# A decoder step on one core: cache pages copied to a DRAM buffer by SyncE instead of gathered by GpSimd

## The chip, the cores and the metric

The kernel runs on 1 core of one Trainium2 chip. The metric is the device time of one execution in microseconds (us), the median of 3 runs. The engines are named as in the profile: PE (TensorE matmuls), PEld (its weight loads), DVE (VectorE), ACT (ScalarE), POOL (GpSimd), SP (SyncE, which here only issues transfers).

## The reference

The reference is one inference step of a two-layer decoder for one prompt of 256 tokens and 8 samples of 4 new tokens each, so 288 tokens in all. A layer is

```
x = x + 1/2 * SwiGLU1(RMSNorm(x))
h = RMSNorm(x);  p = h @ w_in
branches on h: gated DeltaNet | short conv | MLA | memory cross-attention
x = x + W_o( sum_b sigmoid(gate_b(h)) * branch_b )
x = x + 1/2 * SwiGLU2(RMSNorm(x))
```

The part that the change is about is the MLA branch of the samples. Each sample has a past of 2048 tokens in 16 pages of 128 tokens, found through a page table:

```
c_all = concat([ckv_pool[layer, pages].reshape(-1, 256), c_new])   # latent keys/values
r_all = concat([kr_pool[layer, pages].reshape(-1, 32),  r_new])    # rope keys
k = rmsnorm(concat([c_all @ w_uk per head, r_all]))                # 8 heads
p = softmax(q . k * scale, masked);  out = (p @ c_all) @ w_uv
```

All is fp32; the layers' outputs, the new states and the new cache rows are returned.

## The kernel before

Every large product is made of three fp32r matmuls: operands are split into a high and a low part, and `mm3` (L261 to L263) adds high·high, low·high and high·low. The weights come as 470 raw tiles `wraw` of 128x1024 (512 KB). SP loads them in a fixed order (`Stream.load`, L146) into four buffers; ACT makes the high part `wh` (L159) and DVE the low part `wl` (L160). So the weight stream passes SP, ACT and DVE ahead of each matmul on PE, and a raw tile is loaded as soon as DVE has made the last `wl` from the tile four before it.

A layer has these stages (times of layer 0 in the trace): FFN1 (7 to 215 us), stage AB with the memory branch and the convolutions (215 to 390), stage C with the MLA projections and the prompt's attention (390 to 525), stage D with the delta rule and the samples' paged attention (526 to about 935), then `wo` and FFN2. Layer 1 lies 1194 us later. A list of steps per stage is interleaved by hand, and a scheduler then orders the instructions of each engine by data and by its own estimate of when each is ready; so a change of what one engine issues can change the order on others.

What the prediction speaks of:

- `mem_prep` (L423 to L442), at the start of AB, loads the memory's eight tiles `mt` (128 KB each, two buffers, L426). For each, ACT makes `mh`, DVE makes `ml` (L429) and adds its square to `macc` (L241); L437 sums `macc` on PE. A tile's load has to wait until the tile two before it has been read.
- `mem_values` (L556 to L566), at the end of AB, loads for each of 8 samples a 512-KB tile `kc` (L561, two buffers), and PE makes 8 small matmuls with it into `accp` (L566).
- In D each page is used twice. Its transposed form `ct` (256 gathers of 128 KB) and the rope keys `kT` (64 gathers of four pages) are fetched by `page_fetch` (L1094) as indirect transfers issued by POOL (L1091). ACT and DVE split `ct` into `ch` and `cl`, and PE makes the keys `pgps`. The plain form `cn` is loaded by SP through `load_page` (L1203), with the page's number read into a register first.
- Every transfer of SP stands in one queue, in order, and takes one of eight semaphores in turn (DMAHW0 to DMAHW7), each free again when the transfer eight before has landed.

Of the kernel before, what the change touches and what calls it, by code (L numbers as in the profile page):

```python
# [28 lines left out]
PT, PSUB = T + 4, SUB + 4  # L29

# [3 lines left out]
    ("blk4", 4), ("i32s", 32), ("bmp", 8), ("hm", 4), ("sel", 2), ("cs", T), ("kt", T), ("iota", 1), ("iota32", 1),  # L34
# [98 lines left out]
class Stream:  # L133


    def __init__(self, nc, raw_pool, split_pool, dram, plan, ahead=3, raw_ahead=3):
        self.nc, self.rp, self.sp, self.dram, self.plan = nc, raw_pool, split_pool, dram, plan
        self.pos = self.n_sub = self.n_raw = 0
        self.ahead, self.raw_ahead = ahead, raw_ahead
        self.raw, self.sub = {}, {}  # L140
        self.total_raw = dram.shape[0]

    def load(self, upto):
# [34 lines left out]
def program(tc, I, O):  # L178
# [15 lines left out]

    base = pool("base")
# [121 lines left out]

    def ffn(n, ka, kb, nxt):
# [3 lines left out]
        for j in range(NFF):  # L322
            pg = proj(ka, j, KD, n.hi, n.lo)
            g = mk(fp, [128, T], "fg", bufs=2)
            mul(g, pg, n.r)
            act(g, g, AF.Silu)
            pu = proj(ka, NFF + j, KD, n.hi, n.lo)
            u = mk(fp, [128, T], "fu", bufs=2)
            mul(u, pu, n.r)
            mul(u, u, g)  # L330
            split(ah[:, j, :], al[:, j, :], u)
        ins = nc.scalar.preload_act_table_set("natural_log_exp_and_others")
        tc.keep_in_program_order(ins)
        for m in range(KD):
            ps = proj(kb, m, NFF, ah, al)
            STT(out=x[:, m, :], in0=ps, scalar=0.5, in1=x[:, m, :], op0=ALU.mult, op1=ALU.add)
            if nxt is not None:
                nxt.tile(m)
            else:
                nc.sync.dma_start(O["y"][:, m, :], x[:, m, :])  # L340
        fp.release()

    def mix(l, n, nxt):
# [289 lines left out]
        n_phys = I["ct"].shape[0] // (depth * 128)  # L633
        idx, idx4 = mk(ma, [128, NB * NPG], "idx", I32), mk(ma, [128, NB * 4], "idx4", I32)
        off = mk(ma, [128, 2], "off")
        TS_(out=off[:, 0:1], in0=C("iota"), scalar1=float(l * n_phys * 128), scalar2=None, op0=ALU.add)
        TS_(out=off[:, 1:2], in0=C("iota32"), scalar1=float(l * n_phys * 32), scalar2=None, op0=ALU.add)
        TS_(out=idx, in0=pti, scalar1=128.0, scalar2=off[:, 0:1], op0=ALU.mult, op1=ALU.add)
        TS_(out=idx4, in0=pt4, scalar1=32.0, scalar2=off[:, 1:2], op0=ALU.mult, op1=ALU.add)
# [442 lines left out]

        core = delta()
# [111 lines left out]
        loads = []  # L1195

        def load_page(dst, pg):
            ld, (page,) = nc.values_load_multi_w_load_instructions(
                pti[0:1, pg:pg + 1], engines=[mybir.EngineType.SP], min_val=0, max_val=n_phys - 1)
            if len(loads) > 3:  # L1200
                tc.add_manual_dep(ld[0].ins, loads[-4].ins.name, mybir.DependencyInfo(
                    mybir.DependencyClass.NoSync, mybir.DependencyReason.DATA), reason="registers")
            loads.append(nc.sync.dma_start(dst, I["cn"][l, bass.ds(page, 1), :, :].rearrange("o p c -> (o p) c")))  # L1203

        def values(b, qd):
# [7 lines left out]
            for i in range(2):  # L1213
                cn = mk(sa, [128, 2, 257], "cn", bufs=3)
                nc.vector.memset(cn[:, :, 256:257], 1.0)
                for j in range(2):
                    load_page(cn[:, j, 0:256], b * NPG + qd * 4 + i * 2 + j)
# [40 lines left out]

        mhl = []
# [17 lines left out]
    for k in range(KD):  # L1277
        nc.sync.dma_start(x[:, k, :], I["x"][:, k, :])
        if k == 1:
            W.load(1)  # L1280
    n = Norm(0, "g_f1")
# [5 lines left out]
    for m in range(KD):  # L1287
# [3 lines left out]
    pti = mk(base, [128, NB * NPG], "pti", I32)  # L1291
    nc.sync.dma_start(pti, I["pt"].rearrange("(o n) -> o n", o=1).to_broadcast([128, NB * NPG]))

    pt4 = mk(base, [128, NB * 4], "pt4")
    pt4t = mk(base, [128, NB * 4, 4], "xs")
    TT(out=pt4t, in0=pti.rearrange("p (q j) -> p q j", j=4), in1=C("blk4").unsqueeze(1).to_broadcast([128, NB * 4, 4]),
       op=ALU.mult)
    nc.vector.tensor_reduce(out=pt4, in_=pt4t, axis=AX.X, op=ALU.add)
    n.finish()
    for l in range(depth):  # L1300
# [11 lines left out]
    for p in (psb, psa, psm, wsp, wraw, base):  # L1312
# [3 lines left out]
def constants():  # L1316
# [41 lines left out]
    c["iota"][:, 0] = i  # L1358
    c["iota32"][:, 0] = i % 32
# [5 lines left out]
def layout(a):  # L1365
# [58 lines left out]
    f["ct"] = ct.reshape(-1, 256)  # L1424
    f["krt"] = a["cache_mla_krope"].transpose(0, 1, 3, 2).reshape(-1, 128)
# [46 lines left out]
```

## Time and profile before

| | |
|---|---|
| runs | 2417.37, 2409.87, 2414.66 us; median 2414.66 |
| profiled execution | 2407.3 us, its span 2405.3 us |
| mean granted clock of PE | 0.99 |
| busy share of the span | PE 96%, PEld 90%, DVE 66%, ACT 55%, POOL 15% |
| chain that ended last | PE 91%, DVE 3%, ACT 2%, DMA 2%, issue 2% |
| DMA | 149 GB/s over the span |

PE is busy nearly all the time, so the table alone says little about a change that touches no matmul. The profile has to be read by stage: where PE has gaps, how long each is, and which engine or transfer ended it. In the windows PEclk is the granted clock as a share of the full one.

### The profile page before, as it was taken

What the parts mean: (1) busy time and instruction counts of PE and PEld (TensorE: products, weight loads), DVE (VectorE), ACT (ScalarE), POOL (GpSimd) and SP (SyncE); (2) the same over time, 40 slices, a digit from 0 to 9 for tenths busy, and PEclk for the clock granted to TensorE, in tenths of its full rate; (3) what the DMA queues carried; (4) which work ended last, traced back from release to release, by engine and by line L of the source; (5) the groups of instructions that cost most, each with busy time, mean ns of one, the idle gap of its engine ahead of it and who ended that gap; (6) DMA issues with size and microseconds to landing.
All of it is one profiled execution on the core that took longest, in us unless ns stands there. A gap on an engine that the chain in (4) does not pass through costs nothing.

```text
span 2405.3 us, 50145 instructions
## 1 busy us (share of the span) xinstructions
PE 2310.6 (96%) x18368; PEld 2153.4 (90%) x18368; DVE 1597.9 (66%) x3484; ACT 1333.8 (55%) x3489; POOL 350.8 (15%) x461
## 2 busy tenths in 40 slices
PE   8999999999889999999999999999998899999999
PEld 8999898978767888999999998998887678889999
DVE  6666897675556655766566668876754666567664
ACT  5555756754445655655455557566544466556553
POOL 0000110113334430000000001101133344200000
PEclk9999999999999999999999999999999999999999
DMA  6555655431244445555555556553322444355554
GB/s 235 167 167 179 211 180 177 123 118 52 82 138 133 123 135 159 162 167 167 167 167 167 167 171 219 192 166 116 116 60 75 151 121 138 118 154 162 167 170 136
DMA packets 134949, 359.16 MB, mean 149 GB/s; under 512 B 19312, under 2 KB 56880, under 8 KB 134704
## 3 DMA queue, kind: packets, MB, share of 16 engines
q1 hardware_dynamic: 120368, 318.19, 42.2%
q0 software_dynamic: 14336, 37.77, 5.5%
q8 instruction: 146, 2.39, 0.4%
q14 instruction: 99, 0.81, 0.1%
HBM read 346.82 MB, written 9.06 MB: 148 GB/s over the span
## 4 chain that ended last, share of the span: by engine, by line
PE 91%; DVE 3%; ACT 2%; DMA 2%; issue 2%; another core or an unknown queue 0%; SPq 0%; ACTq 0%; DVEq 0%
PE mmps L261 20%; PE mmps L262 20%; PE mmps L263 19%; PE pgps L261 6%; PE pgps L263 6%; PE pgps L262 5%; PE accp L1220 2%; PE axp L864 2%; DMA mt<-in_mem 1%; PE axp L683 1%; ACT wh L159 1%; PE axp L1164 1%; DVE mx L1177 1%; PE axp L371 0%; DMA kc<-in_mem_v 0%
## 5 line engine op out<-in xcount | busy, mean ns | idle before, releaser
L159 ACT CAST wh<-wraw 128x512 fp32r<-128x512 f32 x940 | 580.1, 619 | 607.2 <-PE mmps L262 551.2
L160 DVE TENSOR_TENSOR wl<-wraw,wh 128x512 fp32r<-128x512 f32 x940 | 648.3, 691 | 344.9 <-ACT wh L159 296.6
L261 PE MATMUL mmps<-xh,wh 128*128 128x288 f32 x2512 | 751.6, 299 | 9.1 <-ACT wh L159 8.0
L262 PE MATMUL mmps<-xl,wh 128*128 128x288 f32 x2512 | 748.5, 298 | 0.0
L263 PE MATMUL mmps<-xh,wl 128*128 128x288 f32 x2512 | 741.9, 295 | 0.1
L261 PEld LDWEIGHTS mmps<-xh,wh 128*128 128x128 f32 x2512 | 473.7, 189 | 22.5 <-ACT wh L159 10.8
L262 PEld LDWEIGHTS mmps<-xl,wh 128*128 128x128 f32 x2512 | 475.2, 189 | 3.5 <-issue 1.4
L263 PEld LDWEIGHTS mmps<-xh,wl 128*128 128x128 f32 x2512 | 474.5, 189 | 3.5 <-issue 1.6
L261 PE MATMUL pgps<-mvh,ch 128*128 128x272 f32 x1024 | 316.7, 309 | 28.5 <-ACT s L1156 22.2
L1091 POOL DMA_INDIRECT ct<-in_ct,idx x256 | 249.3, 974 | 582.0 <-DVE cl L258 161.7
L244 ACT ACTIVATE sq<-pgps 128x256 f32<-128x256 f32 x512 | 193.6, 387 | 221.4 <-PE pgps L263 165.6
L262 PE MATMUL pgps<-mvl,ch 128*128 128x272 f32 x1024 | 301.2, 294 | 0.0
L263 PE MATMUL pgps<-mvh,cl 128*128 128x272 f32 x1024 | 300.9, 294 | 0.0
L261 PEld LDWEIGHTS pgps<-mvh,ch 128*128 128x128 f32 x1024 | 196.6, 192 | 63.6 <-ACT s L1156 35.6
L1157 DVE TENSOR_REDUCE ssum<-sq 128x8 f32<-128x512 f32 x256 | 173.6, 680 | 110.6 <-ACT sq L244 99.0
L261 PE MATMUL mmps<-ah,wh 128*128 128x288 f32 x704 | 207.7, 295 | 0.0
L263 PE MATMUL mmps<-ah,wl 128*128 128x288 f32 x704 | 207.6, 295 | 0.0
L262 PE MATMUL mmps<-al,wh 128*128 128x288 f32 x704 | 207.3, 294 | 0.0
L262 PEld LDWEIGHTS pgps<-mvl,ch 128*128 128x128 f32 x1024 | 197.1, 193 | 2.4 <-issue 1.4
L263 PEld LDWEIGHTS pgps<-mvh,cl 128*128 128x128 f32 x1024 | 196.4, 192 | 2.1 <-issue 0.7
L261 PEld LDWEIGHTS mmps<-ah,wh 128*128 128x128 f32 x704 | 132.4, 188 | 0.0
L262 PEld LDWEIGHTS mmps<-al,wh 128*128 128x128 f32 x704 | 132.4, 188 | 0.0
(407 smaller groups left out, 3376.6 us busy)
## 6 DMA issues: line engine op xcount, KB each, us to landing
wraw<-in_w SPq DMA_DIRECT2D x470, 512.0 KB
cn<-in_cn SPq DMA_DIRECT2D x256, 128.0 KB
kc<-in_mem_k SPq DMA_DIRECT2D x16, 512.0 KB
kc<-in_mem_v SPq DMA_DIRECT2D x16, 512.0 KB
ct<-in_ct,idx POOLq DMA_INDIRECT x256
S<-in_dn_S SPq DMA_DIRECT2D x8, 512.0 KB
out_s_S<-S SPq DMA_DIRECT2D x8, 512.0 KB
mt<-in_mem SPq DMA_DIRECT2D x16, 128.0 KB
```

The lines of the kernel that those rows point to most:

```text
L159: nc.scalar.copy(h, src)
L160: nc.vector.tensor_tensor(out=lo, in0=src, in1=h.bitcast(F32), op=ALU.subtract)
L244: nc.scalar.activation(out=out, in_=in_, func=f, **kw)
L261: MMUL(ps, wh, xh, start=first, stop=False)
L262: MMUL(ps, wh, xl, start=False, stop=False)
L263: MMUL(ps, wl, xh, start=False, stop=last)
L683: MMUL(p2, C("ones96"), sq, start=True, stop=True)
L864: MMUL(dst[sl, h, :], lhs[sl, h, :], rhs[sl, :] if rhs is identc else rhs[sl, h, :], start=True, stop=True)
L1091: nc.gpsimd.indirect_dma_start(out=dst, out_offset=None, in_=src, in_offset=bass.IndirectOffsetOnAxis(ap=ix, axis=0))
L1157: nc.vector.tensor_reduce(out=ssum[:, pg, :], in_=sq.rearrange("p a (h e) -> p (a h) e", e=64), axis=AX.X, op=ALU.add)
L1164: MMUL(prp[:, 0:128], kT4, qbd.rearrange("p g j -> p (g j)"), start=True, stop=True)
L1220: MMUL(ppc[32 * j:32 * j + 32, :], s[:, qd * 4 + j, :], cns[j // 2][:, j % 2, :], start=qd == 0 and j > 0, stop=qd == 3)
```

## The change

For each layer a DRAM buffer `rec` of 128 records is made. A record has a page's transposed latent part and its rope keys side by side: 16 rows of 2304 floats, 147,456 bytes. The host lays the cache out in such records (`ct`, with the rope keys at the end). `page_copies` copies the 128 pages in the order of the page table, each with a register load and one transfer from DRAM to DRAM, issued by SP. `copy_pages` is called after each raw tile's load (`Stream.beside`) and issues one or two copies up to raw tile 70 (three for two tiles), one for two tiles from 70 to 127, and one for each tile from 128 on; layer 0's copies begin in FFN1, layer 1's behind stage D of layer 0.

In D the 256 gathers of `ct` become 128 loads of two pages each (256 KB), and the 64 gathers of rope keys become 64 loads of four pages (64 KB), both from `rec`, issued by SP. POOL issues no transfer any more. The loads of `cn` stay, now through `page_load`, which the copies use too. The page table is loaded once into one partition, and the DVE instructions that worked out the gathers' indices go. In the FFNs DVE and ACT take the program's order instead of the scheduler's. PE has the same matmuls.

```
+    def page_load(pg, moves):
+        ld, (page,) = nc.values_load_multi_w_load_instructions(
+            pti[0:1, pg:pg + 1], engines=[mybir.EngineType.SP], min_val=0, max_val=n_phys - 1)
...
+        for dst, src in moves:
+            d = nc.sync.dma_start(dst, src[bass.ds(page, 1)].rearrange("o p c -> (o p) c"))
+    def page_copies(l):
+        rec = copied[l] = dram.tile([NB * NPG, 16, PREC // 16], F32, tag=f"rec{l}", name="rec")
+        for pg in range(NB * NPG):
+            page_load(pg, ((rec[pg], I["ct"][l]),))
+            yield
+    def copy_pages(n):
+        for _ in range(1 + (n < 70 and n % 2) - (70 <= n < 128 and n % 2)):
+            if next(held_copies[0], 0) == 0:
+                return
...
             self.n_raw += 1
+            if self.beside is not None:
+                self.beside(self.n_raw)
...
+        with tc.manual_schedule(engines={mybir.EngineType.Activation, mybir.EngineType.DVE}):
+            for j in range(NFF):
...
-        def gather(dst, src, ix):
-            nc.gpsimd.indirect_dma_start(out=dst, out_offset=None, in_=src,
-                                         in_offset=bass.IndirectOffsetOnAxis(ap=ix, axis=0))
+        rec = copied.pop(l).rearrange("n a b -> n (a b)")
...
-                gather(kT4, I["krt"], idx4[:, n // 2:n // 2 + 1])
+                nc.sync.dma_start(kT4, rec[2 * n:2 * n + 4, 128 * 256:].rearrange("g (d t) -> g d t", t=128))
             ct = held["ct", n] = mk(sa, [128, 2, 256], "ct", bufs=3)
-            for j in range(2):
-                gather(ct[:, j, :], I["ct"], idx[:, 2 * n + j:2 * n + j + 1])
+            nc.sync.dma_start(ct, rec[2 * n:2 * n + 2, 0:128 * 256].rearrange("g (p c) -> p g c", c=256))
```

The change also moves instructions in layer 0 where no source line is edited; in layer 1's AB the order is the one of before. On DVE at the start of AB of layer 0, before:

```order
L160 TENSOR_TENSOR wl_2863<-wraw_2606,wh_2862 128x512 [waits Activation_49]
L160 TENSOR_TENSOR wl_2881<-wraw_2640,wh_2880 128x512 [waits DMAHW4_49,PE_49,Activation_49]
L238 TENSOR_TENSOR mq_2741<-mmps_2861,nr_2702 128x288 [waits PE_49]
L160 TENSOR_TENSOR wl_2907<-wraw_2640,wh_2906 128x512 [waits Activation_49]
L429 SCALAR_TENSOR_TENSOR ml_2729<-mt_2764,par_82,mh_2728 128x256 [waits DMAHW3_49,Activation_49]
L241 TENSOR_TENSOR macc_2730<-macc_2730,t_2768 128x256 [waits DVE_49,Activation_49]
L429 SCALAR_TENSOR_TENSOR ml_2729<-mt_2771,par_82,mh_2728 128x256 [waits DMAHW4_49,Activation_49]
L241 TENSOR_TENSOR macc_2730<-macc_2730,t_2775 128x256 [waits DVE_49,Activation_49]
L160 TENSOR_TENSOR wl_2925<-wraw_2674,wh_2924 128x512 [waits DMAHW5_49,PE_49,Activation_49]
```

and now:

```order
L243 TENSOR_TENSOR cin_4137<-mmps_4140,nr_3771 128x256 [waits PE_49]
L243 TENSOR_TENSOR cin_4137<-mmps_4140,nr_3771 128x8x4
L257 TENSOR_SCALAR csg_4341<-csg_4341 128x312 [waits Activation_49]
L514 TENSOR_SCALAR cacc_4465<-cin_4137,par_84 128x312 [waits DVE_49,Pool_49]
L463 SCALAR_TENSOR_TENSOR ml_3798<-mt_3833,par_84,mh_3797 128x256 [waits DMAHW3_49,Activation_49]
L246 TENSOR_TENSOR macc_3799<-macc_3799,t_3837 128x256 [waits Activation_49]
L463 SCALAR_TENSOR_TENSOR ml_3798<-mt_3840,par_84,mh_3797 128x256 [waits DMAHW4_49,Activation_49]
L246 TENSOR_TENSOR macc_3799<-macc_3799,t_3844 128x256 [waits DVE_49,Activation_49]
L516 SCALAR_TENSOR_TENSOR cacc_4465<-cin_4137,par_84,cacc_4465 128x312
```

Before, the second pair of `ml` (from mt_2764 and mt_2771) stands between weight splits. Now the second pair (mt_3833, mt_3840) stands behind the first convolution tile (`cin`, `cacc`), which needs PE's product mmps_4140; the loads of the third pair, mt_3847 and mt_3854, wait for these two `ml`.

On PE at the end of AB of layer 0, the matmuls with the last four `kc` tiles, before (the first two of them):

```order
L566 MATMUL accp_4330<-kc_4797,pm_4799 32x128 [waits DMAHW3_49,DVE_49]
L523 MATMUL axp_4743<-cst_73,mp_4738 128x128 [waits DVE_49,Activation_49]
L523 MATMUL axp_4743<-cst_73,mp_4738 128x128
L523 MATMUL axp_4743<-cst_73,mp_4738 128x128 [waits Activation_49]
L523 MATMUL axp_4743<-cst_73,mp_4738 128x128
L566 MATMUL accp_4330<-kc_4797,pm_4799 32x128 x7
L566 MATMUL accp_4330<-kc_4809,pm_4811 32x128 [waits DMAHW5_49]
L566 MATMUL accp_4330<-kc_4809,pm_4811 32x128 x4
L528 MATMUL axp_4750<-mpT_4748,mV_2737 128x256 [waits Activation_49]
L528 MATMUL axp_4750<-mpT_4748,mV_2737 128x256
L566 MATMUL accp_4330<-kc_4809,pm_4811 32x128 x3
L511 MATMUL axp_4821<-mK_2736,mq_2741 128x256 x2
```

and now, all four:

```order
L266 MATMUL mmps_6300<-xh_169,wh_6239 128x288
L267 MATMUL mmps_6300<-xl_170,wh_6239 128x288
L268 MATMUL mmps_6300<-xh_169,wl_6240 128x288
L600 MATMUL accp_5575<-kc_6086,pm_6088 32x128 [waits DMAHW2_49,DVE_49]
L600 MATMUL accp_5575<-kc_6086,pm_6088 32x128 x7
L600 MATMUL accp_5575<-kc_6098,pm_6100 32x128 [waits DMAHW3_49,DVE_49]
L600 MATMUL accp_5575<-kc_6098,pm_6100 32x128 x7
L600 MATMUL accp_5575<-kc_6134,pm_6136 32x128 [waits DMAHW5_49,DVE_49]
L600 MATMUL accp_5575<-kc_6134,pm_6136 32x128 x7
L600 MATMUL accp_5575<-kc_6146,pm_6148 32x128 [waits DMAHW6_49,DVE_49]
L600 MATMUL accp_5575<-kc_6146,pm_6148 32x128 x7
L606 MATMUL axp_6160<-cst_75,mot_6158 128x128 [waits Activation_49]
```

Before, other products stood between the tiles: of the memory branch between the first two, as shown, and of the projections behind them. Now their 32 matmuls stand in one row, while the buffers for `kc` are still two.

On SP at the start of D of layer 0, now:

```order
L148 DMA wraw_8041<-in_w 128x1024 [waits DMAHW2_49,DVE_49]
L148 DMA wraw_8084<-in_w 128x1024 [waits DMAHW3_49,DVE_49]
L148 DMA wraw_12250<-in_w 128x1024 [waits DMAHW4_49,DVE_49]
L1128 DMA kT4_8108<-rec_198 128x1x128
L1130 DMA ct_8110<-rec_198 128x2x256 [waits PE_49]
L1130 DMA ct_8112<-rec_198 128x2x256
L1128 DMA kT4_8120<-rec_198 128x1x128
L1130 DMA ct_8122<-rec_198 128x2x256 [waits DMAHW5_49]
L1128 DMA kT4_8296<-rec_198 128x1x128 [waits DMAHW6_49]
L1128 DMA kT4_8461<-rec_198 128x1x128 [waits DMAHW1_49,DMAHW7_49,PE_49,Activation_49]
```

The first page loads stand behind the load of wraw_12250, which waits on DVE (for the last `wl` of stage C). Before, POOL issued the first gathers of D by itself, eight of them from 470.9 to 481.3 us.

## Rows read from the trace of the kernel before

**Rows 1.** The page's first part: busy time, share of the span, instructions.

```profile
PE 2310.6 (96%) x18368; PEld 2153.4 (90%) x18368; DVE 1597.9 (66%) x3484; ACT 1333.8 (55%) x3489; POOL 350.8 (15%) x461
```

**Rows 2.** Busy time by engine in stretches of 60 us.

```profile
core 0: us, PE busy (x) PEld busy (x) DVE busy (x) ACT busy (x) POOL busy (x), PEclk, DMA share, GB/s
...
60.00:120.00 60.00, 60.00 (x457) 60.00 (x457) 41.37 (x76) 30.03 (x56) 0.00 (x0) 1.00 0.54 167
...
180.00:240.00 60.00, 58.59 (x440) 58.00 (x438) 38.07 (x73) 33.55 (x65) 1.58 (x12) 1.00 0.58 179
...
660.00:720.00 60.00, 49.99 (x471) 41.46 (x471) 36.08 (x103) 25.52 (x109) 22.70 (x26) 0.95 0.43 138
720.00:780.00 60.00, 55.42 (x419) 46.04 (x420) 36.19 (x94) 33.25 (x134) 25.86 (x27) 0.93 0.44 134
...
1800.00:1860.00 60.00, 53.66 (x575) 45.54 (x573) 28.73 (x68) 25.76 (x101) 18.93 (x20) 0.91 0.26 75
```

**Rows 3.** Chain that ended last: start us, us, what; pieces without a releaser.

```profile
631.52 2.53 another core or an unknown queue
...
648.81 1.41 another core or an unknown queue
...
712.48 1.74 another core or an unknown queue
...
1823.68 2.57 another core or an unknown queue
```

**Rows 4.** Timeline of POOL: start us, us, instruction, idle before and releaser.

```profile
632.27 0.95 POOL L1091 DMA_INDIRECT ct<-in_ct,idx  x1 [0.30 <-issue]
```

**Rows 5.** DMA queues from 631.3 to 634.3 us: packets, MB, share.

```profile
q0 software_dynamic: 110, 0.31, 36.0%
```

**Rows 6.** Chain that ended last: its pieces of transfers.

```profile
221.40 3.34 DMA mt<-in_mem
225.87 2.61 DMA mt<-in_mem
228.91 4.66 DMA mt<-in_mem
234.70 2.40 DMA mt<-in_mem
...
370.32 6.04 DMA kc<-in_mem_v
...
1567.25 4.79 DMA kc<-in_mem_v
```

**Rows 7.** Costliest groups, two of DVE: busy, mean ns of one, idle before.

```profile
L160 DVE TENSOR_TENSOR wl<-wraw,wh 128x512 fp32r<-128x512 f32 x940 | 648.3, 691 | 344.9 <-ACT wh L159 296.6
...
L429 DVE SCALAR_TENSOR_TENSOR ml<-mt,par,mh 128x256 fp32r<-128x256 f32 x16 | 7.7, 481 | 3.6 <-ACT mh L244 3.5
```

**Rows 8.** Timeline of PE: a wait for kc, and one for DVE.

```profile
376.49 0.97 PE L566 MATMUL accp<-kc,pm 128*32 128x128 f32 x10 [2.24 <-DMA kc<-in_mem_v]
...
715.61 1.22 PE L1052 MATMUL axp<-vx,bd 32*128 32x256 f32 x4 [4.21 <-DVE uq L241]
```

**Rows 9.** Short stretches behind these two waits, columns as in rows 2.

```profile
376.00:378.00 2.00, 1.51 (x13) 1.11 (x14) 0.00 (x0) 0.00 (x0) 0.00 (x0) 0.64 0.82 321
378.00:380.00 2.00, 2.00 (x13) 1.29 (x12) 0.53 (x4) 0.85 (x2) 0.00 (x0) 0.51 0.07 28
...
716.00:718.00 2.00, 2.00 (x9) 1.35 (x8) 1.44 (x5) 0.60 (x4) 0.00 (x0) 0.50 0.21 74
...
722.00:724.00 2.00, 2.00 (x29) 1.13 (x18) 1.81 (x6) 0.40 (x1) 0.00 (x0) 0.50 0.00 0
```

**Rows 10.** Timeline of SP: page loads with their register loads.

```profile
599.72 2.00 SPq L1203 DMA_DIRECT2D cn<-in_cn  x4
```

**Rows 11.** Timeline of PE around the start of stage D.

```profile
525.69 0.29 PE L263 MATMUL mmps<-boh,wl 128*128 128x288 f32 x1
...
529.23 0.40 PE L261 MATMUL pgps<-mvh,ch 128*128 128x272 f32 x1
```

More of the change, by code (lines that the diff above doesn't have):

```diff
@@ L141, in __init__ @@
         self.total_raw = dram.shape[0]
+        self.beside = None
     def load(self, upto):
@@ L193, in mk @@
         return p.tile(shape, dt, tag=name, name=name, **kw)
+    dram = tc.alloc_tile_pool(name="dram", bufs=1, space=bass.MemoryType.DRAM)
     base = pool("base")
@@ L316, in finish @@
             return self
+    n_phys = I["ct"].shape[1]
+    loads, copied = [], {}
+    def page_load(pg, moves):
+        ld, (page,) = nc.values_load_multi_w_load_instructions(
+            pti[0:1, pg:pg + 1], engines=[mybir.EngineType.SP], min_val=0, max_val=n_phys - 1)
+        if len(loads) > 3:
+            tc.add_manual_dep(ld[0].ins, loads[-4].ins.name, mybir.DependencyInfo(
+                mybir.DependencyClass.NoSync, mybir.DependencyReason.DATA), reason="registers")
+        for dst, src in moves:
+            d = nc.sync.dma_start(dst, src[bass.ds(page, 1)].rearrange("o p c -> (o p) c"))
+        loads.append(d)
+    def page_copies(l):
[7 more added lines that the diff above has]
+                return
+    held_copies = []
     def ffn(n, ka, kb, nxt):
@@ L321, in ffn @@
         al = mk(fp, [128, NFF, PT], "al", F32R)[:, :, :T]
[L322 to L340, printed above, removed]
+        with tc.manual_schedule(engines={mybir.EngineType.Activation, mybir.EngineType.DVE}):
+            for j in range(NFF):
+                pg = proj(ka, j, KD, n.hi, n.lo)
+                g = mk(fp, [128, T], "fg", bufs=2)
+                mul(g, pg, n.r)
+                act(g, g, AF.Silu)
+                pu = proj(ka, NFF + j, KD, n.hi, n.lo)
+                u = mk(fp, [128, T], "fu", bufs=2)
+                mul(u, pu, n.r)
+                mul(u, u, g)
+                split(ah[:, j, :], al[:, j, :], u)
+            ins = nc.scalar.preload_act_table_set("natural_log_exp_and_others")
+            tc.keep_in_program_order(ins)
+            for m in range(KD):
+                ps = proj(kb, m, NFF, ah, al)
+                STT(out=x[:, m, :], in0=ps, scalar=0.5, in1=x[:, m, :], op0=ALU.mult, op1=ALU.add)
+                if nxt is not None:
+                    nxt.tile(m)
+                else:
+                    nc.sync.dma_start(O["y"][:, m, :], x[:, m, :])
         fp.release()
@@ L1081, in delta @@
             dn.release()
+        W.beside = None
+        for _ in held_copies[0]:
+            pass
         core = delta()
@@ L1193, in softmax @@
             st[b] = (s, pn)
[L1195 to L1203, printed above, removed]
         def values(b, qd):
@@ L1257, in mix @@
         ma.release()
+        if l + 1 < depth:
+            held_copies[0] = page_copies(l + 1)
+            W.beside = copy_pages
         mhl = []
@@ L1280, in program @@
             W.load(1)
+    pti = mk(base, [1, NB * NPG], "pti", I32)
+    nc.sync.dma_start(pti, I["pt"].rearrange("(o n) -> o n", o=1))
     n = Norm(0, "g_f1")
@@ L1290, in program @@
     nc.sync.dma_start(msk, I["msk"])
[L1291 to L1298, printed above, removed]
     n.finish()
+    held_copies.append(page_copies(0))
+    W.beside = copy_pages
     for l in range(depth):
@@ L1311, in program @@
             n.finish()
-    for p in (psb, psa, psm, wsp, wraw, base):
+    for p in (psb, psa, psm, wsp, wraw, base, dram):
         p.release()
```

19 lines of the change are left out of this document (6 added, 13 removed).

## The prediction

> **What bounds the kernel now.** The page's first part comes first: PE is busy 96% of the span [rows 1], so an edit counts only by what it adds to or takes from PE's gaps. The stretches of 60 us show where gaps are. In the FFN (60 to 120 us) PE is busy 60.00 of 60 with 457 matmuls, 131 ns each, and the transfers take 0.54 of the DMA engines: there is nothing to gain there, and room beside it. At the start of stage AB (180 to 240) 1.41 us are idle. Stage D is the weak place: 10.01 us idle in 660 to 720, 4.58 in the next stretch, with a granted clock of 0.95 and 0.93; layer 1 has 6.34 us and 0.91 at 1800 [rows 2].
>
> The chain of waits says what ends these gaps. At three places of D in each layer a piece of it has no releaser: 2.53, 1.41 and 1.74 us in layer 0, 5.7 together, and the same places in layer 1, of which the first (2.57) is shown; 11.4 in all [rows 3]. At the first, DVE starts 2.5 us late, and POOL has just issued gathers [rows 4]; at all six POOL is in a run of them. The other pieces that matter are transfers at the start of AB (`mt`) and at its end (`kc`) [rows 6]. PE waited 2.24 us for `kc` in layer 0 [rows 8].
>
> [...]
>
> **What costs nothing.** The program order in the FFNs, the POOL instructions and the DVE index arithmetic that go: PE has no gap there [rows 2]. The page loads within D: POOL ran ahead of their use by many microseconds and SP's queue still does, two or three buffers deep; the loads of `cn` stay as they were. The cover is the distance between load and use, 12 us or more by the instruction order and 0.13 us per matmul; without it each of 128 loads would show its landing.
>
> The copies: SP spends about 0.5 us on a page's register load and issue [rows 10], so 1.5 copies cost 0.75 us of the 3.14 us in which PE uses up one raw tile (24 matmuls of 131 ns). On the DMA engines, a raw tile of 512 KB has 0.54 of them now; 1.5 copies are 221 KB, which is 0.23 more if only the bytes read count, and 0.47 if bytes read and written each count: 0.77 to 1.01. I take the lower end at no cost, since raw tiles are loaded up to four ahead and at 0.77 the queue drains.
>
> **What is late, all in layer 0.** (1) *Start of AB.* The second pair of `ml` now stands on DVE behind the first convolution tile, and the loads of the third pair wait for it, those of the fourth for the third. From that tile's last product, five DVE instructions of up to 0.48 us [rows 7] make about 2.3 us. A pair's cycle, issue to issue, was 3.0 us (225.87 to 228.91) or 5.8 (228.91 to 234.70); the last pair takes its landing, 2.4 to 4.7, and 1.0 for `mh` and `ml` [rows 6]. Together 2.3 + 3.0 + 3.4 = 8.7 up to 2.3 + 5.8 + 5.7 = 13.8 us, while PE has 46 matmuls, 6.0 us, up to the last use. That is a wait of 2.7 to 7.8 instead of 1.4: +1.3 to +6.4, I take the middle, +4.
>
> (2) *End of AB.* The last four `kc` tiles are used in one row, through two buffers. The third can be asked for when the first has been used, so two pairs of landings stand one behind the other. A pair needs 4.8 to 6.0 us from its first issue [rows 6]; two need 9.6 to 12.0. Against that PE has about 2.7 us of other products between the buffers' release and the first of the four, and 0.6 of its own: a wait of 6.3 to 8.7, or 5.6 if the pairs overlap in part. Before it was 2.24: +3.4 to +6.5, I take +5. Behind it nothing else is late, since raw tiles were loaded meanwhile.
>
> (3) *Start of D.* SP's first page loads stand behind a raw load that waits for the last `wl` of stage C. From the product before it: three DVE instructions no longer than a `wl` (1.6), the `wl` (0.69, [rows 7]), three issues of up to 0.5 us [rows 10] (1.2), a landing as of `mt`, 2.4 to 4.7 [rows 6], and ACT's split, as long as a `wl`: 6.6 to 8.9 us. PE has 3.5 us from that product to its first page product (525.69 to 529.23, [rows 11]), and some 2.0 of prompt attention that now stand in between: +1.1 to +3.4, I take +2. In layer 1 PE has about 3 us more work there, and I take 0. Queued behind that raw load on SP are only page loads and `cn`.
>
> Together +11 (5.8 to 16.3).
>
> (4) *The clock.* The waits of (1) and (2) are then 5 to 8 us, as long as the 4.21-us one. Each may bring some 4.5 us at half clock, of which `kc` already pays 1.7 [rows 9]: 0 to 7.3, I take +4, nearer to the one wait of their length.
>
> (5) *The gathers that go.* The three unexplained waits per layer (11.4) may go with them, and the clock lost in these stretches: (0.05 + 0.07) x 60 in layer 0 and 0.09 x 60 in layer 1, 12.6 us [rows 2, 3]. So 0 to -24. The two readings below can't be told apart from this trace; I take half of the waits and none of the clock, -6.
>
> Sum: 11 + 4 - 6 = +9 us against the profiled execution's 2407.3 us (span 2405.3), which lies 7.4 under the median of the runs, 2414.66. Added to the median: **2424 us**.
>
> **The rivals.** (A) *The gathers caused all late starts: faster.* For it: each of the six falls into a run of gathers, at the same program places in both layers; and between 631.3 and 634.3 us the only packets on the DMA queues were of the software queue, 110 of them at 36% [rows 5], so no engine was then having instructions loaded. Against it: one late start was ACT's (648.8), and at most other gathers nothing is late. Price: 11.4 + 12.6 go, +11 and half of the clock (2) come: 2414.66 - 11 = 2404 us. It decides from the point where more than 20 us of the 24 go, at the waits as I took them.
> [...]
> [...]
>
> (B) *No change.* `mt` and `kc` land at their fast ends, the short matmuls in the waits keep the clock up, and half of the late waits go: 5.8 + 0 - 6 = 0, so 2412 to 2420. For it: the 1.41 us idle at 180 to 240 left the clock at 1.00 [rows 2]. Against it: the distances above are short even so.
>
> (C) *The copies starve the weight stream: much slower.* If writing to DRAM costs three times a read, 1.5 copies take 0.70, the engines would need 1.24 of their time, and 70 raw tiles in layer 0 would come 70 x 3.14 x 0.24 = 53 us late, less a cover of about 16 us (four raw buffers and the split tiles behind them, some five tiles): +37, 2452 us or more. It decides from a share of 1.0. Against it: even both bytes counted end at 1.01, and layer 1's copies are one per tile.
>
> **How the numbers follow.** My forecast has a chance of 0.45, A 0.28, B 0.17, C 0.10. A measurement of this kernel can tell about 0.3%, 7.2 us, from no change. My case has its own range from 2414 to 2436 (the sum's waits and clock at either end, with -6): slower 0.36, same 0.09. A is faster in 0.24, same in 0.04; B same 0.12, faster 0.03, slower 0.02; C slower 0.10. So slower 0.48, same 0.25, faster 0.27. The lowest sum, 5.8 + 0 - 24, is 2396, the highest without C, 16.3 + 7.3, is 2438; with a part of A and of C left out the range is 2399 to 2440.
>
> **What the new profile would show.** (1) PE waiting for DVE (`ml` or `macc`) 3 to 8 us near 225 us, and in layer 1 as before. (2) PE waiting for `kc` in layer 0 at two or three places, 6 to 9 us in all, in layer 1 about 1 as before. (3) PE waiting 1 to 3 us ahead of the first `pgps` in layer 0. (4) A clock near 0.9 in a stretch behind (1) or (2). (5) The pieces without a releaser at 631, 649 and 712 us gone, or there. FFN stretches at 60.00 with a DMA share near 0.77 show the copies hidden; a gap with `wraw` as its releaser shows C. I am wrong if the waits of (1) and (2) together stay under 5 us, if D gets shorter by more than 10 us per layer, or if the FFN has gaps.

## The result, and the profile after

The changed kernel takes 2348.18 us (median of four runs, 2346.36 to 2348.84) against 2413.61 (2409.87 to 2417.37) for the kernel before on the same chip: a ratio of 0.976 [0.973, 0.979], faster by 65 us. The forecast was 2424. The profiled execution's span went from 2405.3 to 2347.1 us. The page's first part, after, for [rows 1]:

```profile
span 2347.1 us, 51350 instructions
...
PE 2295.0 (98%) x18368; PEld 2148.8 (92%) x18368; DVE 1598.1 (68%) x3474; ACT 1321.6 (56%) x3489; POOL 33.7 (1%) x141
```

PE's busy time alone fell by 15.6 us, with as many matmuls. Some 10 of these are the clock: its mean rose from 0.990 to 0.994, which is 24 us of full clock lost before (0.010 x 2405.3) and 14 now. The next view is the busy time by engine in stretches, of the kernel before: from the end of FFN1 to PE's first page product, then stage D of layer 0 and of layer 1, each from its first page product to its last (start:end, length, busy us and instructions of each engine, granted clock, DMA share, GB/s).

```profile
core 0: us, PE busy (x) PEld busy (x) DVE busy (x) ACT busy (x) POOL busy (x), PEclk, DMA share, GB/s
215.00:529.20 314.20, 306.06 (x2254) 279.42 (x2252) 243.01 (x580) 206.03 (x479) 28.39 (x73) 0.99 0.53 166
529.20:915.80 386.60, 351.94 (x3190) 307.40 (x3190) 227.25 (x553) 198.42 (x776) 146.72 (x154) 0.98 0.38 112
1723.50:2111.30 387.80, 355.14 (x3189) 309.01 (x3189) 227.35 (x553) 198.54 (x776) 146.79 (x154) 0.97 0.37 111
```

The same three of the kernel after, between the same places of the program:

```profile
215.00:567.10 352.10, 323.40 (x2286) 291.88 (x2284) 247.12 (x588) 205.07 (x485) 12.83 (x65) 0.96 0.53 167
567.10:908.00 340.90, 336.25 (x3178) 298.51 (x3179) 225.17 (x544) 202.43 (x774) 0.43 (x2) 1.00 0.42 128
1713.60:2052.40 338.80, 335.97 (x3183) 298.85 (x3183) 226.45 (x551) 202.68 (x776) 0.88 (x2) 1.00 0.43 130
```

These rows hold the whole result. The stretch up to the first page product is 37.9 us longer; D is 45.7 us shorter in layer 0 and 49.0 in layer 1. The rest (between the two D's and behind the second) makes -1.4, and the sum is the span's -58.2. In D, 59.8 us of idle PE time went (34.7 to 4.6 and 32.7 to 2.8, each the length less PE's busy time) and 34.9 us of busy time. The clock, 0.98 and 0.97 before and 1.00 now, gives some 19 of these (0.02 x 386.6 + 0.03 x 387.8 = 19.4). The other 15 or so go with the number of gaps: PE had 47 in each D and has 13 and 10 now. In a row, matmuls of 0.29 us start 0.13 apart. Around the wait that ended at 234.06 us of the kernel after, the last matmul before it counts with its full 0.29, and the second one behind it starts 0.23 after the first. That makes 0.26 us more busy time for a gap, or 18 for the 71 that went (an estimate).

PE's order of instructions in D of layer 0 is nearly the same in both kernels (2187 of its 2197 rows; ACT's 745 of 749), so the gain is not a better order. What PE waited for there, before (engine, line, what it waited for: us in total, times, longest):

```profile
PE pgps L261 <- ACT s L1156: 11.0, 10, 2.5
PE axp L1052 <- DVE uq L241: 4.2, 1, 4.2
PE axp L864 <- issue: 3.5, 5, 1.1
PE axp L1180 <- DVE mx L1177: 3.5, 5, 0.9
```

And after:

```profile
PE accp L1237 <- DMA cn<-in_cn: 1.4, 2, 1.3
PE axp L1207 <- DVE mx L1204: 1.3, 4, 0.4
PE axp L1069 <- DMA S<-in_dn_S: 0.9, 1, 0.9
PE pgps L266 <- ACT ch L262: 0.8, 1, 0.8
```

The waits that went were put down to ACT and DVE, which the change left as they were. The timelines of before tell more. ACT, DVE and POOL in one place of layer 0's D:

```profile
702.44 0.38 ACT L244 ACTIVATE sq<-pgps 128x256 f32<-128x256 f32 x1 [4.35 <-PE pgps L263]
```

```profile
699.80 1.12 DVE L1057 SCALAR_TENSOR_TENSOR S<-S,bb,axp 128x128 f32<-128x128 f32 x4
702.37 0.42 DVE L241 TENSOR_TENSOR uq<-uq,axp 128x256 f32<-128x256 f32 x1 [1.45 <-PE pgps L263]
```

```profile
699.54 0.94 POOL L1091 DMA_INDIRECT ct<-in_ct,idx  x1 [2.23 <-issue]
700.79 0.94 POOL L1091 DMA_INDIRECT ct<-in_ct,idx  x1 [0.30 <-issue]
```

Both `sq` and `uq` wait for PE; `uq` needs the products of L1042, whose record ends at 700.55. ACT and DVE start together, 0.07 us apart and 1.8 us after that end, when POOL has just issued a gather. Counted over D of layer 0 by the timelines (an ACT or DVE start 0.25 to 4 us after the end of the last instruction of the PE line that released it; PE's ends are modelled), 50 of 241 such releases were late before, 29.5 us together, and 3 of 283 after, 1.2 us.

The trace also says behind which gathers. POOL issues them alone or in rows, in a row 0.3 us apart, as the two above. Counted record by record (the timelines merge some, which adds a few late ones), 97 releases were late in the two D's of before, and all 97 stand during a gather that follows another in a row, or up to 1.5 us after its end (97 of 262 releases there). Behind a gather that came alone or first in its row none of 42 was late, and farther from any gather none of 185.

In the stretch that got longer, PE's waits after were these (the same columns):

```profile
PE mmps L268 <- DVE wl L164: 8.5, 10, 2.0
PE mmps L266 <- ACT wh L163: 6.8, 6, 2.5
PE accp L600 <- DMA kc<-in_mem_v: 6.5, 4, 2.8
PE mmps L267 <- DVE ml L463: 1.4, 1, 1.4
```

Beside the `kc` that was forecast, PE waits 15.3 us for weight splits. What the splits themselves waited for from 215 to 425 us, after (engine sat idle until: us, times):

```profile
its engine sat idle before it (us, times) until:
  PE mmps L267: 14.0, 15
  ACT wh L163: 5.0, 6
  DMA wraw<-in_w: 0.6, 1
```

The transfers cost 0.6 us: the tiles had landed, and the splits stood too late in ACT's and DVE's own order. So it was at the longest of these waits, 2.47 us up to 247.25, on ACT:

```profile
244.46 0.46 ACT L249 ACTIVATE csg<-cacc 128x312 f32<-128x312 f32 x1 [6.68 <-DVE cacc L516]
...
246.59 1.12 ACT L163 CAST wh<-wraw 128x512 fp32r<-128x512 f32 x2
```

ACT waited 6.68 us for a convolution tile, with the `wh` that PE needed behind it; at 310.02 (5.35 us) and 358.99 (6.50 us) the same. Only 1362 of PE's 1805 rows in this stretch of layer 0 stand as before; in layer 1 it is 1782. The clock followed the gaps, 0.94 and 0.91 where PE idled 6.3 and 9.8 us of 60. In stretches of 60 us, after, for [rows 2]:

```profile
60.00:120.00 60.00, 60.00 (x453) 60.00 (x453) 41.38 (x75) 28.81 (x57) 0.00 (x0) 1.00 0.78 233
...
180.00:240.00 60.00, 58.24 (x436) 57.64 (x435) 32.81 (x58) 28.78 (x54) 0.99 (x10) 1.00 0.62 192
240.00:300.00 60.00, 53.67 (x328) 46.22 (x327) 47.52 (x115) 40.31 (x98) 5.84 (x24) 0.94 0.64 207
300.00:360.00 60.00, 50.23 (x329) 45.05 (x327) 40.20 (x95) 23.48 (x49) 4.75 (x24) 0.91 0.53 174
...
660.00:720.00 60.00, 59.00 (x589) 50.85 (x589) 39.27 (x107) 32.24 (x130) 0.43 (x2) 1.00 0.38 116
720.00:780.00 60.00, 57.42 (x490) 47.36 (x489) 41.96 (x111) 37.07 (x146) 0.00 (x0) 1.00 0.54 166
...
1800.00:1860.00 60.00, 59.64 (x607) 51.80 (x607) 38.58 (x101) 34.06 (x137) 0.88 (x2) 1.00 0.36 108
```

FFN1 is full at a DMA share of 0.78 (0.54 before): the copies are hidden there.

### The profile page after: what moved, and what is told of

Its sections match the earlier page's. It is cut to its first block, busy times and chain, and to the rows that moved or that the text cites. A ratio compares the mean times of both kernels' runs of the same rounds, so it can differ in the third digit from the quotient of the medians.

```text
span 2347.1 us, 51350 instructions
## 1 busy us (share of the span) xinstructions
PE 2295.0 (98%) x18368; PEld 2148.8 (92%) x18368; DVE 1598.1 (68%) x3474; ACT 1321.6 (56%) x3489; POOL 33.7 (1%) x141
## 4 chain that ended last, share of the span: by engine, by line
PE 92%; DVE 3%; ACT 2%; DMA 2%; issue 1%; SPq 0%; DVEq 0%; ACTq 0%
PE mmps L266 21%; PE mmps L268 20%; PE mmps L267 20%; PE pgps L266 6%; PE pgps L268 5%; PE pgps L267 5%; PE accp L1237 2%; PE axp L891 2%; PE axp L710 1%; PE axp L1191 1%; DMA kc<-in_mem_v 1%; PE axp L405 1%; DVE mx L1204 0%; ACT wh L163 0%; DVE wl L164 0%
## 5 line engine op out<-in xcount | busy, mean ns | idle before, releaser
L164 DVE TENSOR_TENSOR wl<-wraw,wh 128x512 fp32r<-128x512 f32 x940 | 633.5, 689 | 265.4 <-ACT wh L163 251.3
L163 ACT CAST wh<-wraw 128x512 fp32r<-128x512 f32 x940 | 563.4, 616 | 277.3 <-PE mmps L267 255.3
L266 PE MATMUL pgps<-mvh,ch 128*128 128x272 f32 x1024 | 308.4, 301 | 0.9 <-ACT ch L262 0.8
L262 ACT CAST ah<-fu 128x288 fp32r<-128x288 f32 x88 | 38.1, 433 | 175.1 <-DVE fu L243 175.1
L263 DVE TENSOR_TENSOR cl<-ct,ch 128x512 fp32r<-128x512 f32 x128 | 88.1, 689 | 68.3 <-ACT ch L262 59.3
```

The source lines that it names most:

```text
L163: nc.scalar.copy(h, src)
L164: nc.vector.tensor_tensor(out=lo, in0=src, in1=h.bitcast(F32), op=ALU.subtract)
L262: nc.scalar.copy(hi, src)
L263: TT(out=lo, in0=src, in1=hi.bitcast(F32), op=ALU.subtract)
L266: MMUL(ps, wh, xh, start=first, stop=False)
```

## The experiments

Two things had to be separated: what made D shorter, and what made AB longer. The theory: POOL's gathers delay the releases by PE (rival: something else that changed in D, as the loads from `rec` or SP's queue), and the copies that stand beside AB make the scheduler order it worse (rival: the copies' traffic). Each ratio is to the kernel before on the same chip. The experiments ran on chips 3, 14, 6 and 1 (which of them, or another, the first chip was, that of the result, is not known), and that turned out to matter: the kernel before took about 2404 to 2421 us on the first chip and on chips 3 and 1, but 2303 to 2308 on chips 14 and 6.

**Chip 3** (kernel before: 2420.92 us).

*e1_copies_ffn1*: all copies of layer 0 within FFN1.

```
-        for _ in range(1 + (n < 70 and n % 2) - (70 <= n < 128 and n % 2)):
+        for _ in range(2 if n < 128 else 1):
```

> All 128 copies of layer 0 are issued within FFN1 (two per raw tile up to raw tile 128) and none in stage AB. Theory 1 (the copies' place in AB made the scheduler order AB's splits, mt and kc worse; their traffic is not the point): the stretch from 215 us to the first page product of layer 0 goes from 352 back to 314 to 322 us, in all 2310 to 2322 us, FFN1 without gaps. Rival (the FFNs' program order is what reordered AB): stays at 2348. Rival (the copies' traffic): FFN1 at two copies per tile has a DMA share near 0.86 and gaps of over 5 us with the raw tile's split as releaser.

2312.29 us, ratio 0.955 [0.951, 0.959], in the expected range; 36 us under the change on the first chip, and 35 on one and the same chip (f2 and f3 below). Stretches of this run, the one up to the first page product and one in FFN1:

```profile
215.00:526.00 311.00, 307.17 (x2281) 280.99 (x2280) 245.24 (x584) 207.00 (x484) 21.56 (x65) 1.00 0.56 179
60.00:120.00 60.00, 60.00 (x454) 60.00 (x453) 40.62 (x74) 28.90 (x57) 0.00 (x0) 1.00 0.83 251
```

The stretch is 3.2 us shorter than before the change, and 1652 of PE's 1805 rows stand as before. FFN1 has no gap at a share of 0.83, and the stretch has a share of 0.56 where the change has 0.53, so traffic was not the loss. AB's loss came from the copies that stood beside it in the program, and went with them.

*e2_gathers_back*: the change, but `ct` and `kT` fetched by POOL's gathers again (copies kept).

```
-                nc.sync.dma_start(kT4, rec[2 * n:2 * n + 4, 128 * 256:]...)
+                gather(kT4, I["krg"], idx4[:, n // 2:n // 2 + 1])
...
-            nc.sync.dma_start(ct, rec[2 * n:2 * n + 2, 0:128 * 256]...)
+            for j in range(2):
+                gather(ct[:, j, :], I["ctg"], idx[:, 2 * n + j:2 * n + j + 1])
```

> The changed kernel, but D's ct and kT are fetched by the 320 gathers on POOL again; the copies stay and nobody reads them. Theory 1 (the gathers on POOL hold up DVE and ACT all through D): each stage D goes from 340 back to about 387 us, in all 2430 to 2445 us. Rival (D became faster by something else: its orders, the clock after another start, pages that come earlier): D stays within 10 us of 340 and the total under 2370.

2468.36 us, 1.019 [1.016, 1.023], above the expected range. D is long again, 392.2 us (PE busy 355.09) in layer 0 and 399.1 in layer 1, with 39 of 247 releases late; its chain has eight pieces without a releaser as in [rows 3], the change's has none. Two of them:

```profile
674.38 2.63 another core or an unknown queue
...
806.20 3.82 another core or an unknown queue
```

So the gathers alone bring D's time back, on this chip.

*e5_pool_direct*: the loads from `rec` issued by POOL instead of SP.

```
-            nc.sync.dma_start(ct, rec[2 * n:2 * n + 2, ...])
+            nc.gpsimd.dma_start(ct, rec[2 * n:2 * n + 2, ...])
```

(`kT4` likewise.)

> The changed kernel, but the 128 page loads and 64 rope loads from the records are issued by POOL as plain transfers, no indices. Theory 1a (any transfer that POOL issues costs, by its descriptors): D is slower by 15 to 45 us per layer, 2380 to 2440 us. Theory 1b (only the indexed gathers cost): D within 5 us of the changed kernel's, 2343 to 2358.

2356.41 us, 0.973 [0.969, 0.977]. D takes 345.8 and 345.3 us, 4.4 and 3.3 more than in e1 on the same chip (5 and 6.5 more than with SP on the first); 2 of 285 releases are late in layer 0. In both layers 54 of these transfers stand as close behind another as the gathers of a row do, and none of 92 releases behind them is late. That POOL issues transfers is not what was dear; transfers by an index list are.

*e6_no_copies*: no `rec`; SP loads each page straight from the cache with a register load, as it does `cn`.

```
-            nc.sync.dma_start(ct, rec[2 * n:2 * n + 2, 0:128 * 256]...)
+            for j in range(2):
+                page_part(2 * n + j, ((ct[:, j, :], 0, 128 * 256, 256),
+                                      (kT4[32 * g:32 * g + 32, :], 128 * 256, PREC, 128)))
```

> No copies at all: SP loads ct and the rope keys straight from the cache page by page, with a register load each (256 more in D, two transfers each). Theory 1: AB of layer 0 has the order of before, so 35 us come back there, and D stays at about 340: 2308 to 2320 us. Rival (SP's queue in D gets late by 128 register loads and 256 transfers per layer, some 100 us more of SP's time): D slower by 5 to 30 us per layer with ct or wraw as releaser, 2325 to 2375.

2392.84 us, 0.989 [0.985, 0.993], outside both ranges. The stretch up to the first page product is as short as in e1 (309.3 us, and 311.0), which fits the first finding, but D takes 376.8 and 380.3. PE idles only 14.6 us of it; its order in D is another one (964 of 1995 rows as before), and the value products, 392 ns each in both, cover 37.6 us of PE's time by themselves against 20.1 in e1. That the scheduler's order does this is argued from these counts; SP's queue as its cause was not shown.

**Chip 14** (before: 2303.06 us). These runs were to show what of a gather costs.

*e3_half_gathers*: every other `ct` gathered by POOL, the others by SP.

```
+            if n % 2 == 0:
+                nc.sync.dma_start(ct, rec[2 * n:2 * n + 2, 0:128 * 256]...)
+            else:
+                for j in range(2):
+                    gather(ct[:, j, :], I["ctg"], idx[:, 2 * n + j:2 * n + j + 1])
```

> The changed kernel with half of D's ct tiles (the odd ones, 64 gathers per layer) fetched by POOL's gathers, the others and all rope keys by SP from the records. If each gather costs by itself: 64 of 160 per layer, D slower by 0.4 of what the full set cost (51 and 60 us), so about 20 to 25 us per layer, 2388 to 2405 us in all. If only runs of three to five gathers behind one another cost: D slower by under 8 us per layer, under 2370.

*e4_pool_compute*: the change, and POOL copies 128x256 values four times per `ct` (its result is not used).

```
+            for j in range(4):
+                nc.gpsimd.tensor_copy(out=dump, in_=held["ct", n][:, j % 2, :])
```

> The changed kernel with four copies of 128x256 by POOL for each ct tile in D (256 per layer, no transfer by POOL), so POOL is about as busy as with the gathers. If POOL's work in SBUF is what holds up the others: D slower by 15 us or more per layer, and DVE's own instructions longer. If it takes the gathers: D within 6 us per layer, 2348 to 2360 us.

*e9_narrow_gathers*: after SP's load of a `ct`, two gathers of 128 rows x 64 values over it, so as many gathers with a quarter of the bytes.

```
+            for j in range(2):
+                gather(ct[:, j, 0:64], I["ctg"], idx[:, 2 * n + j:2 * n + j + 1])
```

> The changed kernel; each ct tile, loaded by SP, then gets a quarter of its columns again by two gathers of 128 rows of 256 bytes (128 gathers per layer, a quarter of the bytes). If the gathers' issue and descriptors cost: D slower by 30 to 50 us per layer, 2410 to 2450. If their bytes cost: about a quarter of 50, 10 to 15 us per layer, 2365 to 2380. Against both, the splits would wait for late gathers, with the gather as releaser of ch on ACT.

2350.69 us (1.020 [1.017, 1.024]), 2354.83 (1.022) and 2365.33 (1.027); D takes 341.1, 342.2 and 343.1 us in layer 0. None shows a price of gathers, and none settles anything by itself, since here the kernel before, with all its gathers, is 118 us faster than on chip 3.

*e10_e1_ffn_scheduled*: e1 without the program order in the FFNs.

```
-        with tc.manual_schedule(engines={mybir.EngineType.Activation, mybir.EngineType.DVE}):
+        if True:
```

> The first experiment's kernel (copies of layer 0 all in FFN1) without the FFNs' program order for ACT and DVE. Theory: PE has no gaps in the FFNs in either order, so 2312 within 4 us. Rival: the order in the FFNs carries some of the gain at their borders: 2318 to 2330.

2791.91 us, 1.211 [1.208, 1.215], far outside both ranges. Over the span PE waits 241.6 us in 136 waits for `wh`, and FFN1 has gaps:

```profile
60.00:120.00 60.00, 42.70 (x209) 38.57 (x210) 19.89 (x37) 13.24 (x27) 0.00 (x0) 0.80 0.38 120
```

In the same 60 us ACT waited for these (engine, line, what it waited for: us in total, times, longest):

```profile
ACT ah L262 <- DVE fu L243: 26.9, 5, 6.0
ACT fg L249 <- DVE fg L243: 21.6, 4, 5.5
```

The DMA share is 0.38, and no split waited for a transfer: with two copies beside each raw tile the scheduler puts the splits behind instructions of ACT that wait for DVE. The program order is needed there.

**Chip 6** (before: 2306.0 us). Is the difference one of the chip?

*f1_before_again*, *f2_after_again*, *f3_copies_ffn1_again*, *f4_narrow_again*: the kernel before, the change, e1 and e9, unedited.

> The kernel before, unchanged, with a profile. In the last four runs, on another chip, it took 2303 us and not 2414. Theory 2 (the gathers' hold-up depends on the chip, the rest of the program does not): either about 2414 with stages D near 387 us and late releases from PE, or about 2303 with stages D near 335 us and none; the stretches outside D the same in both to 3 us. Rival (something else differs between chips, clock or transfers): the missing 111 us are spread over the FFNs too.

> The changed kernel, unchanged. Theory 2: about 2348 us on any chip, as it has no gathers; so faster than before by 2.7% where before takes 2414, and slower by 2% where it takes 2303. Rival: it gains on a fast chip as before does, 2240 us.

> The first experiment's kernel again (layer 0's copies all in FFN1). Theory 2: 2312 us on any chip, so within 0.5% of the kernel before where that takes 2303. Rival as for the changed kernel.

> The changed kernel with 128 narrow gathers per layer beside the page loads, again. On a chip where before takes 2414: if the number of gathers sets the price, D slower by 30 to 50 us per layer, if their bytes do, 10 to 15. Where before takes 2303: about 2365 as in the last run, with D within 5 us of the changed kernel's.

2303.52, 2349.32 (1.019 [1.016, 1.022]), 2314.29 (1.005 [1.003, 1.006]) and 2363.67 (1.026). The change takes the time that it took on the first chip; the kernel before does not. The two D stages of the kernel before on this chip:

```profile
523.10:868.80 345.70, 339.56 (x3189) 301.86 (x3189) 227.53 (x553) 202.64 (x776) 148.00 (x154) 0.99 0.41 125
1670.60:2013.00 342.40, 337.45 (x3189) 299.47 (x3189) 227.33 (x553) 202.59 (x776) 148.06 (x154) 1.00 0.41 126
```

The same 154 POOL instructions take 148 us (146.7 and 146.8 on the first chip), but D is 41 and 45 us shorter than on the first chip, 4 of 270 releases are late, and the chain has no piece without a releaser. Of the 98 us by which the span is shorter (2405.3 to 2307.2), 86 lie in the two D's; 12 lie outside them, where 3 had been expected, and 6 of these in the stretch ahead of the first, which holds the row of eight gathers from 470.9 us: PE's wait at 486.04, 3.9 us for `psm` on the first chip, is 0.2 here.

So the stretch up to the first page product can be compared on one chip on which gathers cost little, before (f1) and after (f2):

```profile
215.00:523.10 308.10, 305.26 (x2260) 279.77 (x2258) 243.36 (x580) 205.96 (x479) 29.12 (x73) 0.99 0.54 170
215.00:566.50 351.50, 322.27 (x2276) 289.99 (x2275) 246.58 (x586) 203.95 (x483) 13.16 (x65) 0.96 0.52 166
```

The change costs 43.4 us there, not 37.9, and with all copies in FFN1 (f3) the stretch takes 315.2, which is 7.1 more than before.

**Chip 6 again** (before: 2308.33 us). *g1_half_again*, *g2_narrow_third* and *g3_pool_compute_again* are e3, e9 and e4; *g4_e1_gathers* is e1 with all gathers, as in e2.

> The changed kernel with the odd ct tiles by gathers (64 per layer), again. Where before takes about 2414: if the number counts, D 20 to 25 us longer per layer, 2388 to 2405; if only runs of gathers close behind one another cost, under 2370. Where before takes about 2303: 2350 as before, D at 341.

> The changed kernel with 128 narrow gathers per layer, again. Where before takes about 2414: if the number counts, D 35 to 45 us longer per layer, 2430 to 2455; if the bytes, 10 to 15 us, 2380 to 2395. Where before takes about 2303: 2364.

> The changed kernel with 256 POOL copies per layer in D. 2352 to 2358 on either kind of chip if it takes a gather; D 15 us or more longer per layer where before takes 2414 if POOL's work in SBUF alone is enough.

> Copies of layer 0 all in FFN1, and D's ct and kT by the 320 gathers again. Where before takes about 2414: D at 387 to 399 us, 2410 to 2435 us in all. Where before takes about 2303: D at 341 to 346, 2312 to 2325 us, so the gathers alone cost nothing there.

2350.32, 2362.02, 2351.9 and 2312.44 us (the last 1.002 [1.001, 1.004]). In g4 D takes 345.6 and 340.3 us with all gathers, and 2 of 278 releases are late. Against f3 on the same chip (341.8 and 340.6) the gathers cost D some 4 us in layer 0 and nothing in layer 1; these repeats told nothing new of their price.

**Chip 1** (before: 2403.93 us), a chip that has the price. *h1_half_third* is e3, *h2_narrow_fourth* is e9.

> The changed kernel with 64 gathers of full rows per layer. Where before takes about 2414: number counts, 2388 to 2405; only close runs of gathers cost, under 2370. Where before takes 2303: 2350.

> The changed kernel with 128 narrow gathers per layer. Where before takes about 2414: number counts, 2430 to 2455; bytes count, 2380 to 2395. Where before takes 2303: 2363.

2363.92 us (0.983 [0.978, 0.988]) and 2413.2 (1.004 [1.001, 1.006]). D of layer 0, first with 62 full gathers, then with 123 narrow ones:

```profile
572.10:915.70 343.60, 338.44 (x3178) 301.34 (x3179) 225.43 (x545) 201.02 (x774) 59.82 (x65) 0.99 0.41 126
```

```profile
574.80:941.20 366.40, 346.92 (x3147) 304.96 (x3148) 224.24 (x538) 199.34 (x772) 122.49 (x127) 0.98 0.42 128
```

Against 340.9 and 338.8 us without gathers (the change on the first chip; 338.8 to 342.0 in four runs without them), the 62 cost 3 to 4 us per layer (19 of 269 releases late in layer 0), and the 123 with half as many bytes 23 to 26 (39 of 255 late). h1 fits the range for close gathers; h2 lies between its two. What the gathers carry is not the price. What counts is how many of them follow another in a row, by the count of before, over both layers (late: releases late by more than 0.25 us; longer: the two D's against the change):

| kernel | gathers close behind another | late behind these, of all late | late time (us) | D longer (us) |
|---|---|---|---|---|
| before | 192 | 97 of 97 | 53.2 | 94.7 |
| e2 | 193 | 77 of 79 | 45.8 | 111.6 |
| h2 | 140 | 66 of 70 | 36.4 | 48.4 |
| h1 | 61 | 33 of 33 | 16.2 | 7.0 |
| f1 (chip 6) | 202 | 0 of 0 | 0 | 8.4 |

The late time is 0.24 to 0.28 us per such gather wherever there is a price. D's length is not in proportion to it: in h1 most of it is hidden, and in the others the clock adds to it (0.99 and 1.00 in h1, 0.96 and 0.94 in e2). D stages side by side:

| kernel | chip | gathers in D of a layer | D, layers 0 and 1 (us) |
|---|---|---|---|
| before | first | all | 386.6, 387.8 |
| e2 | 3 | all | 392.2, 399.1 |
| h2 | 1 | 123 narrow | 366.4, 361.7 |
| h1 | 1 | 62 | 343.6, 343.1 |
| after | first | none | 340.9, 338.8 |
| e1 | 3 | none | 341.4, 342.0 |
| f1 | 6 | all | 345.7, 342.4 |
| f2 | 6 | none | 341.8, 339.5 |
| g4 | 6 | all | 345.6, 340.3 |
| e9 | 14 | 123 narrow | 343.1, 342.5 |
| e3 | 14 | 62 | 341.1, 340.0 |

## Why the prediction was wrong

**The step that failed is (5), the gathers that go.** It was sized at -6 us and bounded at -24; measured is -94.7 (45.7 and 49.0), and with it came true one of the signs that the prediction had named for being wrong, a D shorter by more than 10 us. It took the price of the late starts from the chain's pieces without a releaser [rows 3], 11.4 us, and the clock of three stretches [rows 2], 12.6. Measured are 59.8 us of PE's idle time, some 19 of its clock, and some 15 of busy time that went with the gaps. (The chain has five such pieces, 9.6 us; at the sixth place, in layer 1, DVE's 1.77 us are put down to issue.) That half of these waits would go and none of the clock, the -6 of the sum, was the author's choice, which no run shows: the runs show 3 late releases of 283 left in layer 0, and a clock of 1.00 in both D's. The late starts that the view could explain by a semaphore stood in other rows: PE waiting for ACT's `s` or DVE's `uq` [rows 8], which look like slow engines, though these had themselves been released late. Their sum could be read before the change: D's length less PE's busy time was 34.7 us in layer 0 and 32.7 in layer 1. Rival (A) had the mechanism and its place right and used the same price, hence 2404. What was held against it, that at most other gathers nothing is late, looked at the chain alone: 97 releases were late.

A second term was put at nothing: the weight splits in AB, which the change had reordered. They made PE wait 15.3 us, see (1).

The late starts of ACT and of DVE went alike (3 of 283 releases late in layer 0, 50 of 241 before), and ACT had been as late as DVE at 702.4, 0.07 us apart. Nor were they a matter of the instructions by themselves: those of D stayed nearly the same (2187 of PE's 2197 rows and 745 of ACT's 749 in layer 0), and f1, with the very instructions of before, has no piece without a releaser in its chain and 4 of 270 releases late.

**(1) Start of AB: +4.** The wait for `ml` is 1.4 us, as the one for `macc` before. PE had waited 2.47 us for a split shortly before, which gave the loads time; that this is why the wait stayed short is argued, not shown. What was missed is that the splits of the whole stretch had been reordered: 15.3 us. It stood in the same comparison of orders from which the three places were taken.

**(2) End of AB: +5.** Right: four waits for `kc`, 6.5 us in all, where 7.2 (2.24 + 5) had been forecast. PE's timeline after, for [rows 8]:

```profile
413.50 0.64 PE L600 MATMUL accp<-kc,pm 128*32 128x128 f32 x16 [0.40 <-DMA kc<-in_mem_v]
416.92 1.08 PE L600 MATMUL accp<-kc,pm 128*32 128x128 f32 x16 [2.77 <-DMA kc<-in_mem_v]
419.42 1.08 PE L600 MATMUL accp<-kc,pm 128*32 128x128 f32 x16 [1.42 <-DMA kc<-in_mem_v]
422.39 1.08 PE L600 MATMUL accp<-kc,pm 128*32 128x128 f32 x16 [1.88 <-DMA kc<-in_mem_v]
```

**(3) Start of D: +2.** One wait of 0.8 us for `ch`: a little below the range of 1.1 to 3.4.

**(4) The clock: +4.** The direction was right, the size too small: from 240 to 480 us it is 0.94, 0.91, 0.97 and 0.95, which is 13.8 us of 240 by the same working, where 1.7 were lost before [rows 9]. The 4.5 us that (4) has for one wait is an estimate that no run shows as such: before, behind DVE's wait of 4.21 us, the clock was 0.50 from 715.6 to 724 us, which makes 4.2. Of the 13.8 some 5 stand behind the waits for `kc`, as (4) had it for one such wait:

```profile
410.00:420.00 10.00, 5.41 (x78) 4.18 (x80) 3.96 (x9) 1.73 (x3) 0.00 (x0) 0.82 0.73 224
420.00:430.00 10.00, 7.74 (x60) 6.35 (x52) 3.30 (x9) 3.96 (x10) 0.00 (x0) 0.67 0.72 279
```

The rest stand behind the waits for splits of (1), none longer than 2.5 us. Steps (1) to (4) were to bring 15 us and brought 37.9, or 43.4 by f1 and f2. (In the chances, the upper end of the forecast's own range should be 2432 by its terms, 16.3 + 7.3 - 6, and not 2436; nothing hangs on it.)

**What costs nothing.** Right for the copies in FFN1: the share is 0.78 where 0.77 was forecast, which speaks for counting only the bytes read, and rival (C) falls. Not right for the order: e10 shows, for two copies beside a raw tile, that the FFNs' program order is no free edit but the condition under which the copies are free. e1 shows that the loss in AB, too, was one of where the copies stood, so most of the 37.9 us need not have been paid.

**What stays open.** Whether it is PE's signal that comes late or PE itself ends late can't be told, since PE's ends are modelled; releases between ACT and DVE were late in at most 9 of about 100 in any kernel. Why it takes a second gather close behind a first was not found. Nor was it found what differs between the chips: a gather on POOL takes 974 ns on the first chip and 980 on chip 6. POOL's computing was tried only on chips that lack the price.

## What to carry to other kernels

Before pricing an edit that takes away a disturbance, sum the idle time and the lost clock of its whole stage, and ask of each wait put down to an engine whether that engine had itself been released late; the pieces without a releaser were less than a fifth of the idle time here. The extra copies cost nothing in traffic at DMA shares of 0.78 and 0.83 (PE busy 60.00 of 60 us in FFN1), but where a scheduler places instructions by its own estimates, such transfers can move others' order (1362 of PE's 1805 rows in the stretch of layer 0 stood as before), so compare the order of the whole stretch and put the transfers where the order is fixed by hand. Where such gathers must stay, keep them from following each other closely (on the first chip 0 of 42 releases were late behind a gather alone or first in its row); that this alone takes the price away was not tried. A change that takes away a price which only some chips have needs runs on several: the same change is 2.4% faster on one and 1.9% slower on another, and e1 4.5% faster or 0.5% slower.

## What the runs showed of the hardware

- The same kernel with about 150 gathers by POOL in each D takes 2404 to 2421 us on the first chip and on chips 3 and 1, and 2303 to 2308 on chips 14 and 6; the change, without them, takes 2348 on the first chip and 2349 on chip 6.
- The late releases stand behind a gather that follows another 0.3 us after its end: 97 of 97 on the first chip, 33 of 33 and 66 of 70 on chip 1, 77 of 79 on chip 3, 0.24 to 0.28 us of late time for each such gather (chip 6: none late behind 202). Behind a gather alone or first in its row 0 of 42 releases were late on the first chip.
- The price does not go by bytes and not in proportion: 62 full gathers cost 3 to 4 us a layer on chip 1, 123 of a quarter of the size 23 to 26, and all of them some 47 on the first chip.
- POOL's transfers without an index list, some 90 in each D, cost 3 to 4 us a layer on chip 3, with 2 of 285 releases late in layer 0.
- Copies of 147 KB from DRAM to DRAM, two beside each raw tile of 512 KB, left PE's FFN1 without a gap at a DMA share of 0.83.
